# A two-block transformer kernel: bias tables of 384 keys issued from ScalarE's queue, and the activations at eight other distances from the weights

## The chip, the cores and the metric

The kernel runs on one core of a Trainium2 chip. The metric is the device time of one execution in microseconds (us); the kernel before was timed three times. On this core TensorE multiplies, VectorE (DVE), ScalarE (ACT) and GpSimd (POOL) do elementwise work, and DMAs that the queues of SyncE (SP) and ScalarE issue bring the weights from HBM.

## The reference

The activations are 256 tokens by 2048 features, all in float32. Two blocks follow each other.

```python
def first_block(x, c, ...):            # one layer
    mod = silu(c) @ w_ada + b_ada      # 6 vectors of 2048: shifts, scales, gates
    h = rmsnorm(x, g_mix) * (1 + sc1) + sh1
    x = x + gt1 * hybrid_mixer(h, w_in, ..., w_out)          # pooling, 8-head attention, LRU
    h = rmsnorm(x, g_ffn) * (1 + sc2) + sh2
    x = x + gt2 * conv_glu_ffn(h, w_gate, w_up, ..., w_down) # 2048 -> 5632 -> 2048
    return rmsnorm(x, final_g)

def second_block(x, ...):              # two layers
    for l in range(2):
        qa, ka, va, qb, kb, vb, qc, kc, vc = split(rmsnorm(x) @ w_in[l])
        oa = window_attention(qa, ka, va, a_sink[l], t5_table)   # bias depends on key - query
        ob = neighborhood_attention(qb, kb, vb, b_rpb[l])        # bias depends on grid offsets
        oc = axial_global_attention(qc, kc, vc, ...)
        x = x + concat(rmsnorm(oa), rmsnorm(ob), rmsnorm(oc)) @ w_o[l]
        u = relu(rmsnorm(x) @ w_up[l])                           # 2048 -> 8192
        x = x + (u * u) @ w_down[l]                              # 8192 -> 2048
    return rmsnorm(x, norm_final)
```

Nearly all the work is in the products with weights, which are read once each. In `window_attention` the bias of head h for query q and key k is one number per key − query; in `neighborhood_attention` the 256 tokens are 4 rows of 64 columns and the bias depends on the row offset and the column offset.

## The kernel before

**Weights.** A `Unit` is 1024 columns of weights on 128 partitions (two k-tiles of 512 columns, or four of 256). It is loaded to one of 7 `raw` buffers by a DMA that SP issues (line 130), and then split: ScalarE copies it to `whi` in fp32r (line 136), VectorE subtracts to get `wlo` (line 137). There are 3 buffers each of `whi` and `wlo` (`HB`). `Ada` items load the modulation weights through the same `raw` buffers (lines 158 and 162), and VectorE accumulates them (line 171).

**Products.** `mm_b` (lines 332 to 334) does three matmuls for each 128 x 128 block of weights: `whi` against the high part of the activations, `whi` against their low part, `wlo` against the high part. The weights are the stationary operand (loaded by LDWEIGHTS), 256 tokens of activations are the moving one. So a unit is 24 matmuls and 24 weight loads, and each matmul has a new weight load. The moving operands are `xh`/`xl` (the residual stream), `uh`/`ul` (the first block's hidden layer), `u` (two tiles `u0`, `u1`, in each layer of the second block), `mb` and the `xn` tiles (parts of the mixers). `mm_a` (lines 347 to 349) has the roles exchanged: 256 or 512 columns of weights move past 128 tokens of `xh`/`xl`.

**Addresses.** In the built program all `whi` and `wlo` buffers start at byte 192 modulo 512 of a partition, and the 128-column blocks that a weight load reads are 512 bytes long, so every weight load starts at 192 modulo 512. Moving slices are 1024 bytes and start at the tile's own residue. Below, *distance* is the start of the moving operand minus that of the weights, modulo 512 bytes. Before, it is 480 for `xh` and `xl`, 0 for `uh`, `ul`, `u0` and `u1`, 320 for `mb`, 288 for the `xn` tiles; in `mm_a`, moving minus stationary, it is 32.

**Order.** `drive` walks a list of items. It issues the DMA of an item up to 7 `raw` buffers ahead, splits up to 3 units ahead, and then emits the matmuls. After each unit, `step` resumes every active generator once; a `yield` in a generator is thus one unit of TensorE's work. `bias_tables` is such a generator; it is started when the first `down` of the first FFN begins. All instructions of an engine run in the order in which they were emitted, a queue's DMAs too.

**Bias tables.** `bias_tables` writes, in DRAM, `bias_a` (8 heads x 256 queries x 256 keys) from a row of 511 numbers per head, by four DMAs of two heads whose rows each start one number earlier; and `bias_b` for each layer (8 x 256 x 256) by 16 DMAs of 64 x 64 blocks for 8 heads. SP issues them, three units apart (lines 1385 and 1395). In each attention layer `heads2` reads a head's table back to a `bias` tile of 128 x 2 x 256 (line 1562), adds the mask `near` on GpSimd for the b heads (line 1568), and the softmax adds it to the scores (line 1049).

Of the kernel before, what the change touches and what calls it, by code (L numbers as in the profile page):

```python
# [9 lines left out]
F32 = mybir.dt.float32  # L10
F32R = mybir.dt.float32r
AF = mybir.ActivationFunctionType
ALU = mybir.AluOpType
# [4 lines left out]
P = 128  # L18
S = 256
D = 2048  # L20
KT = D // P
# [16 lines left out]
CUT2 = 0, 4, 8, 16  # L38
WORD = "p0 p1 a0 a1 b0 b1 l0 l1 p2 l2 a2 b2 p3 l3 a3 b3 p4 l4 a4 b4"
RRATE = 1  # L40
AHRATE = 1.4
HRATE = 1
WINDOWS = (2, 4, 8, 16)
# [139 lines left out]
def flat(a):  # L183
    return a.rearrange("p a b -> p (a b)")
# [15 lines left out]
class Builder:  # L200
# [100 lines left out]
    def dump(self, name, ap):  # L301
        if name in self.dbg:
            self.nc.gpsimd.dma_start(self.dbg[name], ap)

    def open_pool(self, name):
        cm = self.tc.tile_pool(name=name, bufs=1, reuse_waits="tile")
        self.ph = cm.__enter__()
        self.ph_cm = cm
# [168 lines left out]
    def run(self):  # L477
        tc, nc, io = self.tc, self.nc, self.io
        with ExitStack() as es:
            es.enter_context(tc.manual_schedule())  # L480
            cp = self.cp = es.enter_context(tc.tile_pool(name="cp", bufs=1))
            self.st = es.enter_context(tc.tile_pool(name="st", bufs=1))
            self.ps = es.enter_context(tc.tile_pool(name="ps", bufs=1, space=PSUM))
            self.dr = es.enter_context(tc.tile_pool(name="dr", bufs=1, space=DRAM))
            self.params = cp.tile([P, NPAR], F32, name="params")
            self.ident = cp.tile([P, P], F32, name="ident")
            self.ones = cp.tile([P, P], F32, name="ones")
            self.mhalf = cp.tile([P, 2], F32, name="mhalf")
            self.zero = cp.tile([P, 1], F32, name="zero")
            self.mod = cp.tile([P, 96], F32, name="mod")  # L490
            self.cact = cp.tile([P, 16], F32, name="cact")
            self.gsc = cp.tile([P, 16], F32, name="gsc")
            self.fgg = cp.tile([P, 16], F32, name="fgg")
            self.x = cp.tile([P, KT, S], F32, name="x")
            self.xh = cp.tile([P, KT, S], F32R, name="xh")
            self.xl = cp.tile([P, KT, S], F32R, name="xl")
            self.X = (self.xh, self.xl)
            self.rbc = cp.tile([P, S], F32, name="rbc")
            self.acc = cp.tile([P, 512], F32, name="acc")
            self.rtok = cp.tile([P, 2], F32, name="rtok")  # L500
            self.dg = cp.tile([P, S], F32, name="dg")
            nc.scalar.dma_start(self.params, io["params"])
            nc.scalar.dma_start(self.ident, io["ident"])
            nc.vector.memset(self.ones, 1.0)
            nc.vector.memset(self.mhalf, -0.5)
            nc.vector.memset(self.zero, 0.0)
            self.apc = tc.tile_pool(name="ap", bufs=1, reuse_waits="tile")
            self.ap_ = self.apc.__enter__()
            self.mixer()
            if self.upto >= 2:  # L510
                self.ffn()
            self.lead()
# [529 lines left out]
    def softmax(self, b, sc, pr, bias, sink, free=None):  # L1042

        nc = self.nc
        mx, nm, sm, r = self.small(), self.small(), self.small(), self.small()
        init = BIGNEG if sink is None else sink
        for i in range(2):
            other = self.zero.to_broadcast([P, S]) if bias is None else bias[:, i, :]
            nc.vector.tensor_tensor_reduce(
                pr[:, i, :], sc[:, i, :], other, 1.0, init, ALU.add, ALU.max, mx[:, i : i + 1]  # L1050
            )
        nc.vector.tensor_scalar(nm, mx, -1.0, None, ALU.mult)
        self.put("a", b)
        if free:
            self.put("bias", free)
        yield
        yield
        for i in range(2):
            nc.scalar.activation(pr[:, i, :], pr[:, i, :], AF.Exp, bias=nm[:, i : i + 1], accum_out=sm[:, i : i + 1])
        if sink is not None:  # L1060
# [16 lines left out]
    def fox(self, h):  # L1077

        nc = self.nc
        while "fq" not in self.flags:  # L1080
            yield
        pr = yield from self.take("pr", [P, 2, S])
        for i in range(2):
            nc.gpsimd.tensor_scalar(pr[1][:, i, :], self.causal[:, i, :], self.fq[:, i, h : h + 1], 1.0, ALU.add, ALU.mult)
        b = yield from self.bank()
        sc = b[1].rearrange("p (a k) -> p a k", a=2)
# [4 lines left out]
            )  # L1091
            nc.tensor.matmul(sc[:, i, :], sel, self.fs, start=False, stop=True)
        yield
        yield from self.softmax(b, sc, pr[1], pr[1], None)
        pt = yield from self.take("pt", [P, 2, S])
        b = yield from self.bank()
        self.transpose_p(b[1], pr[1])
# [7 lines left out]
        b = yield from self.bank()  # L1105
        o = b[1][:, :S]
# [4 lines left out]
        if "win" not in self.flags:  # L1111
# [5 lines left out]
            b = None  # L1117
# [11 lines left out]
    def ffn(self):  # L1129
        nc, io = self.nc, self.io  # L1130
        wg, wu, wd = io["w_ffn_gate"][0], io["w_ffn_up"][0], io["w_ffn_down"][0]
        F = {}

        def start():
            self.open_pool("ffnp")
            self.slots["sg"] = deque(range(2))
            ph = self.ph
            F["uh"] = ph.tile([P, KT, S], F32R, name="uh")
            F["ul"] = ph.tile([P, KT, S], F32R, name="ul")
            self.rms_now([self.acc, self.sq], self.rbc)  # L1140
# [178 lines left out]
        for q in range(4):  # L1319
            p = self.prep(q, src, "g_ffn", 48, 64, "fp", "ffn")  # L1320
# [27 lines left out]
    def bias_tables(self):  # L1348
# [3 lines left out]
        def rest(n):  # L1352
            for _ in range(n):
                yield
# [21 lines left out]
        rb = []  # L1376
        for l in range(2):
            rb.append(dr.tile([56, 127], F32, name=f"rb{l}"))
            nc.sync.dma_start(rb[l], rows[l])
        self.bias_a = dr.tile([8, S, S], F32, name="bias_a")  # L1380
        self.bias_b = [dr.tile([8, S, S], F32, name=f"bias_b{l}") for l in range(2)]
        yield from rest(12)
        base = rd[0:1, 255:256]
        for h in range(0, 8, 2):
            nc.sync.dma_start(
                self.bias_a[h : h + 2],
                bass.AP(tensor=base.tensor, offset=base.offset + 511 * h, ap=[[511, 2], [-1, S], [1, S]]),
            )
            yield from rest(3)
        for l in range(2):  # L1390
            for r in range(4):
                for r2 in range(4):
                    o = r2 - r + 3
                    base = rb[l][o : o + 1, 63:64]
                    nc.sync.dma_start(
                        self.bias_b[l][:, r * 64 : (r + 1) * 64, r2 * 64 : (r2 + 1) * 64],
                        bass.AP(tensor=base.tensor, offset=base.offset, ap=[[7 * 127, 8], [-1, 64], [1, 64]]),
                    )
                    yield from rest(3)

    def layer(self, l):
        nc, io = self.nc, self.io
# [149 lines left out]
        def heads2(t, kind, g, table, sink, near, need, values, last):  # L1552
# [5 lines left out]
            bias = [None, None]  # L1558
            if table is not None:
                for a in range(2):  # L1560
                    bias[a] = yield from self.take("bias", [P, 2, S])
                    nc.sync.dma_start(bias[a][1], table(a).rearrange("(b p) k -> p b k", p=P))
                yield
                yield
            if near:
                for a in range(2):
                    n = flat(bias[a][1]).rearrange("p (a c) -> p a c", c=64)
                    nc.gpsimd.tensor_tensor(n, n, L["near"].unsqueeze(1).to_broadcast([P, 8, 64]), ALU.add)
            pr = []
            for a in range(2):  # L1570
                pr.append((yield from self.take("pr", [P, 2, S])))
# [9 lines left out]
            yield  # L1581
            soft = [
                self.softmax(bs[a], sc[a], pr[a][1], bias[a][1] if bias[a] else None, sink(a) if sink else None, bias[a])
                for a in range(2)
            ]
            while soft:
# [200 lines left out]
        def mid():  # L1787
            self.close_pool()
            self.open_pool(f"mlp{l}")
            L["u"] = [self.ph.tile([P, KT, S], F32R, name=f"u{i}") for i in range(2)]  # L1790
            if l == 1:
                L["out"] = self.ph.tile([P, 2, D], F32, name="outt")

# [131 lines left out]
```

## Time and profile before

| | us |
|---|---|
| median of 3 runs | 3380.19 |
| lowest and highest | 3378.25 and 3380.22 |
| profiled execution, its own time | 3380.27 |
| its span (first to last instruction) | 3378.5 |

The three runs lie within 0.06% of each other. In the span TensorE's matmuls are busy 97%, its weight loads 95%, VectorE 62%, ScalarE 46%, GpSimd 9%. Matmuls are pipelined, so a busy TensorE is read by the distance in time from one matmul's start to the next, not by its busy share.

### The profile page before, as it was taken

How to read it: one execution, taken by the hardware profiler on the slowest of the kernel's cores; microseconds unless marked ns; L12 is line 12 of the kernel's file. 1: busy time of each engine (PE TensorE's matmuls, PEld its weight loads, DVE VectorE, ACT ScalarE, POOL GpSimd, SP SyncE). 2: the span in 40 equal slices, each digit the busy share in tenths (PEclk: the TensorE clock that was granted, in tenths of full speed). 3: DMA queues.
4: the chain of work that ended last, by engine and by line, in shares of the span. 5: the costliest groups of instructions: out<-in, count | busy, mean ns of one | idle time of the engine just before them, and what ended most of it. 6: DMA issues, size and time to landing. Idle time of an engine off the chain costs nothing.

```text
span 3378.5 us, 63581 instructions
## 1 busy us (share of the span) xinstructions
PE 3279.3 (97%) x26612; PEld 3196.3 (95%) x26612; DVE 2096.3 (62%) x2661; ACT 1569.5 (46%) x2094; POOL 297.6 (9%) x250
## 2 busy tenths in 40 slices
PE   7989899989999999999999999999999999999998
PEld 6988899989999998889999999999889999999998
DVE  7898887636745568666545454556776655545453
ACT  4436345434434466655434343444764533333334
POOL 0022100000000033111000000002110200000001
PEclk9999999989999999999999999999999999999999
DMA  9987887649866654556666666665455666666663
GB/s 362 338 285 231 303 300 242 187 157 298 290 196 187 188 171 133 168 157 183 185 185 184 184 185 185 184 185 162 144 174 163 182 185 184 186 182 187 183 186 125
DMA packets 390719, 683.93 MB, mean 202 GB/s; under 512 B 40823, under 2 KB 97952, under 8 KB 390176
## 3 DMA queue, kind: packets, MB, share of 16 engines
q1 hardware_dynamic: 390144, 679.56, 65.2%
q8 instruction: 208, 3.41, 0.4%
q14 instruction: 79, 0.65, 0.1%
q10 hardware_dynamic: 288, 0.31, 0.0%
HBM read 677.62 MB, written 8.46 MB: 203 GB/s over the span
## 4 chain that ended last, share of the span: by engine, by line
PE 80%; DVE 3%; DMA 3%; ACT 2%; issue 2%; SPq 0%; POOL 0%; ACTq 0%; DVEq 0%; POOLq 0%
PE pg L332 25%; PE pg L334 25%; PE pg L333 25%; DVE wlo L137 1%; DMA raw<-in_w_ffn_up 1%; PE pa L1578 1%; PE pa L1613 1%; PE pa L1073 1%; ACT whi L136 1%; DVE ada L171 1%; PE pg L347 1%; PE pg L348 1%; PE pg L349 1%; DMA raw<-in_w_ada 0%; DMA raw<-in_w_out 0%
## 5 line engine op out<-in xcount | busy, mean ns | idle before, releaser
L137 DVE TENSOR_TENSOR wlo<-raw,whi 128x1024 fp32r<-128x1024 f32 x1064 | 1318.0, 1240 | 1148.5 <-ACT whi L136 1134.9
L136 ACT ACTIVATE whi<-raw 128x1024 fp32r<-128x1024 f32 x1064 | 1123.3, 1058 | 1607.8 <-PE pg L333 1307.0
L332 PE MATMUL pg<-xh,whi 128*128 128x256 f32 x5184 | 1479.1, 285 | 24.7 <-ACT whi L136 20.3
L334 PE MATMUL pg<-xh,wlo 128*128 128x256 f32 x5184 | 1466.1, 283 | 9.4 <-DVE wlo L137 9.3
L333 PE MATMUL pg<-xl,whi 128*128 128x256 f32 x5184 | 1465.5, 283 | 1.8 <-DVE xl L565 1.1
L332 PEld LDWEIGHTS pg<-xh,whi 128*128 128x128 f32 x5184 | 985.5, 190 | 41.9 <-ACT whi L136 21.9
L334 PEld LDWEIGHTS pg<-xh,wlo 128*128 128x128 f32 x5184 | 985.5, 190 | 13.1 <-DVE wlo L137 12.7
L333 PEld LDWEIGHTS pg<-xl,whi 128*128 128x128 f32 x5184 | 985.6, 190 | 5.8 <-DVE xl L565 2.3
L332 PE MATMUL pg<-u,whi 128*128 128x256 f32 x2048 | 579.9, 283 | 0.0
L334 PE MATMUL pg<-u,wlo 128*128 128x256 f32 x2048 | 579.5, 283 | 0.0
L333 PE MATMUL pg<-u,whi 128*128 128x256 f32 x2048 | 579.5, 283 | 0.0
L333 PEld LDWEIGHTS pg<-u,whi 128*128 128x128 f32 x2048 | 393.1, 192 | 0.0
L334 PEld LDWEIGHTS pg<-u,wlo 128*128 128x128 f32 x2048 | 393.1, 192 | 0.0
L332 PEld LDWEIGHTS pg<-u,whi 128*128 128x128 f32 x2048 | 393.1, 192 | 0.0
L171 DVE SCALAR_TENSOR_TENSOR ada<-raw,cact,ada 128x1024 f32<-128x1024 f32 x180 | 233.7, 1298 | 18.9 <-DMA raw<-in_w_ada 17.9
L397 POOL TENSOR_TENSOR acc<-acc,t 128x512 f32<-128x512 f32 (+1 forms) x73 | 95.9, 1327 | 1360.3 <-ACT t L396 1359.2
L334 PE MATMUL pg<-uh,wlo 128*128 128x256 f32 x704 | 199.3, 283 | 0.0
L332 PE MATMUL pg<-uh,whi 128*128 128x256 f32 x704 | 199.3, 283 | 0.0
L333 PE MATMUL pg<-ul,whi 128*128 128x256 f32 x704 | 199.2, 283 | 0.0
L1809 POOL TENSOR_TENSOR y<-y 128x1024 f32<-128x1024 f32 x32 | 61.7, 1927 | 1200.0 <-ACT u L1808 1200.0
L332 PEld LDWEIGHTS pg<-uh,whi 128*128 128x128 f32 x704 | 135.1, 192 | 0.9 <-issue 0.9
L334 PEld LDWEIGHTS pg<-uh,wlo 128*128 128x128 f32 x704 | 135.1, 192 | 0.2 <-DVE wlo L137 0.2
(310 smaller groups left out, 2559.1 us busy)
## 6 DMA issues: line engine op xcount, KB each, us to landing
raw<-in_w_up SPq DMA_DIRECT2D x256, 512.0 KB
raw<-in_w_down SPq DMA_DIRECT2D x256, 512.0 KB
raw<-in_w_ada SPq DMA_DIRECT2D x192, 512.0 KB
raw<-in_w_in SPq DMA_DIRECT2D x192, 512.0 KB
raw<-in_w_ffn_gate SPq DMA_DIRECT2D x88, 512.0 KB
raw<-in_w_ffn_up SPq DMA_DIRECT2D x88, 512.0 KB
raw<-in_w_ffn_down SPq DMA_DIRECT2D x88, 512.0 KB
raw<-in_w_o SPq DMA_DIRECT2D x64, 512.0 KB
```

The costliest lines, as they stand in the source:

```text
L136: b.nc.scalar.activation(hi[:, :n], self.raw[:, :n], AF.Copy)
L137: b.nc.vector.tensor_tensor(lo[:, :n], self.raw[:, :n], hi[:, :n].bitcast(F32), ALU.subtract)
L171: b.nc.vector.scalar_tensor_tensor(g["acc"], self.raw, cs, g["acc"], ALU.mult, ALU.add)
L332: mm(o, wh, xh[:, k0 + j, :], start=st, stop=False, skip_group_check=True)
L333: mm(o, wh, xl[:, k0 + j, :], start=False, stop=False, skip_group_check=True)
L334: mm(o, wl, xh[:, k0 + j, :], start=False, stop=last and j == u.nk - 1, skip_group_check=True)
L347: mm(o, xh[:, k, tok], wh, start=st, stop=False, skip_group_check=True)
L348: mm(o, xh[:, k, tok], wl, start=False, stop=False, skip_group_check=True)
L349: mm(o, xl[:, k, tok], wh, start=False, stop=last and j == u.nk - 1, skip_group_check=True)
L397: nc.gpsimd.tensor_tensor(acc, acc, t, ALU.add)
L1073: self.nc.tensor.transpose(ps[:, k * S + i * P : k * S + (i + 1) * P], pr[:, i, k * P : (k + 1) * P], self.ident)
L1809: nc.gpsimd.tensor_tensor(flat(y), flat(y), flat(y), ALU.mult)
```

## The change

It has two parts that touch each other only through time.

*Bias tables.* `bias_a` and `bias_b` become 8 x 128 x 384: for each of 128 queries a row of 384 keys, of which the first 128 queries of the sequence read columns 128 to 383 and the last 128 read columns 0 to 255 (`by` in `heads2`). `bias_a` is still written by four DMAs, now of 256 rows of 384 numbers where it was 512 rows of 256; `bias_b` by 12 DMAs a layer where it was 16. ScalarE's queue issues them, four units apart where it was three. The `bias` tile is 128 x 384, read by one row a partition.

*Distances.* In `run`, small constant tiles are moved between the large ones; `uh`, `ul` and the `u` tiles come from `skewed`, which takes a tile that starts at a multiple of 512 bytes, with some unused bytes in front. The new distances, from the addresses of the built program:

| moving operand | before | after |
|---|---|---|
| `xh` | 480 | 64 |
| `xl` | 480 | 448 |
| `uh`, `ul` (first block) | 0, 0 | 384, 416 |
| `u0`, `u1` (second block, layer 0) | 0, 0 | 128, 192 |
| `u0`, `u1` (second block, layer 1) | 0, 0 | 256, 352 |

`mb` and `xn` stay at 320 and 288.

```diff
+WRES = 192
+    def skewed(self, name, skew):
+        n = (WRES + skew) % 512 // 4
+        t = self.ph.tile([P, n + KT * S], F32R, name=name, align_bytes=512)
+        return t[:, n:].rearrange("p (k s) -> p k s", k=KT)
 ...
-            F["uh"] = ph.tile([P, KT, S], F32R, name="uh")
-            F["ul"] = ph.tile([P, KT, S], F32R, name="ul")
+            F["uh"] = self.skewed("uh", 384)
+            F["ul"] = self.skewed("ul", 416)
 ...
-        self.bias_a = dr.tile([8, S, S], F32, name="bias_a")
+        self.bias_a = dr.tile([8, P, 384], F32, name="bias_a")
 ...
-            nc.sync.dma_start(
+            nc.scalar.dma_start(
                 self.bias_a[h : h + 2],
-                bass.AP(tensor=base.tensor, offset=base.offset + 511 * h, ap=[[511, 2], [-1, S], [1, S]]),
+                bass.AP(tensor=base.tensor, offset=base.offset + 511 * h, ap=[[511, 2], [-1, P], [1, 384]]),
             )
-            yield from rest(3)
+            yield from rest(4)
 ...
-            for r in range(4):
-                for r2 in range(4):
+            for r in range(2):
+                for m in range(6):
 ...
-                    bias[a] = yield from self.take("bias", [P, 2, S])
+                    bias[a] = yield from self.take("bias", [P, 384])
 ...
-            L["u"] = [self.ph.tile([P, KT, S], F32R, name=f"u{i}") for i in range(2)]
+            L["u"] = [self.skewed(f"u{i}", ((128, 192), (256, 352))[l][i]) for i in range(2)]
```

The distances change no instruction's place in its engine's order. The bias tables do. These rows are SP's queue of before, where the first block's FFN goes from its first `down` (`in_w_ffn_down`) to the next `gate`/`up` units; `raw` is a weight buffer, `rd` the rows of 511 numbers.

```order
L130 DMA raw<-in_w_ffn_down 128x2x512 x9
L130 DMA raw<-in_w_ffn_gate 128x2x512
L158 DMA raw<-in_w_ada 128x1024
L130 DMA raw<-in_w_ffn_gate 128x2x512
L1385 DMA bias_a<-rd 512x1x256
L130 DMA raw<-in_w_ffn_gate 128x2x512
L158 DMA raw<-in_w_ada 128x1024
L130 DMA raw<-in_w_ffn_gate 128x2x512
L1385 DMA bias_a<-rd 512x1x256
L130 DMA raw<-in_w_ffn_gate 128x2x512
L158 DMA raw<-in_w_ada 128x1024
```

And SP's queue of the change at the same place: only weights are left.

```order
L132 DMA raw<-in_w_ffn_down 128x2x512 x9
L132 DMA raw<-in_w_ffn_gate 128x2x512
L160 DMA raw<-in_w_ada 128x1024
L132 DMA raw<-in_w_ffn_gate 128x2x512 x2
L160 DMA raw<-in_w_ada 128x1024
L132 DMA raw<-in_w_ffn_gate 128x2x512 x2
L160 DMA raw<-in_w_ada 128x1024
```

The four `bias_a` DMAs have left the weights' queue. These rows are ScalarE's of the change, in the same stretch of the program: `whi<-raw` is the copy of a unit's weights, `y` a partial sum of `down`, `sg` the gate.

```order
L138 ACTIVATE whi<-raw 128x1024 x8
L1256 ACTIVATE y_7483<-pg 128x512 x2
L138 ACTIVATE whi<-raw 128x1024 x3
L1394 DMA bias_a<-rd 256x1x384
L138 ACTIVATE whi<-raw 128x1024 x4
L1394 DMA bias_a<-rd 256x1x384
L138 ACTIVATE whi<-raw 128x1024
L1256 ACTIVATE y_7734<-pg 128x512 x2
L138 ACTIVATE whi<-raw 128x1024 x3
L1394 DMA bias_a<-rd 256x1x384
L138 ACTIVATE whi<-raw 128x1024 x4
L1394 DMA bias_a<-rd 256x1x384
```

Each `bias_a` DMA now stands between two of ScalarE's weight copies, four of them apart, and the 24 DMAs of `bias_b` follow in the same way; before, ScalarE had only the copies here.

## Rows read from the trace of the kernel before

**Rows 1.** The page, part 1: busy time and share by engine.

```profile
PE 3279.3 (97%) x26612; PEld 3196.3 (95%) x26612; DVE 2096.3 (62%) x2661; ACT 1569.5 (46%) x2094; POOL 297.6 (9%) x250
```

**Rows 2.** The page, part 5: groups of matmuls: count, busy us, mean ns, idle before.

```profile
L332 PE MATMUL pg<-xh,whi 128*128 128x256 f32 x5184 | 1479.1, 285 | 24.7 <-ACT whi L136 20.3
L332 PE MATMUL pg<-u,whi 128*128 128x256 f32 x2048 | 579.9, 283 | 0.0
L332 PE MATMUL pg<-uh,whi 128*128 128x256 f32 x704 | 199.3, 283 | 0.0
```

**Rows 3.** Timeline, PE: first and last of 99 matmuls with `xh`/`xl`.

```profile
1939.61 0.28 PE L333 MATMUL pg<-xl,whi 128*128 128x256 f32 x1
...
1951.20 0.28 PE L332 MATMUL pg<-xh,whi 128*128 128x256 f32 x1
```

**Rows 4.** Timeline, PE: first and last of 99 matmuls with `u`.

```profile
1849.72 0.28 PE L333 MATMUL pg<-u,whi 128*128 128x256 f32 x1
...
1861.48 0.28 PE L332 MATMUL pg<-u,whi 128*128 128x256 f32 x1
```

**Rows 5.** Timeline, PE: first and last of 99 matmuls with `mb`.

```profile
1549.60 0.28 PE L333 MATMUL pg<-mb,whi 128*128 128x256 f32 x1
...
1561.14 0.28 PE L332 MATMUL pg<-mb,whi 128*128 128x256 f32 x1
```

**Rows 6.** Timeline, PE: first and last of 99 matmuls with `xn`.

```profile
349.83 0.28 PE L333 MATMUL pg<-xn,whi 128*128 128x256 f32 x1
...
361.26 0.28 PE L332 MATMUL pg<-xn,whi 128*128 128x256 f32 x1
```

**Rows 7.** Timeline, PE: first and last of 70 matmuls of `mm_a`, 256 columns.

```profile
2339.44 0.28 PE L349 MATMUL pg<-whi,xl 128*128 128x256 f32 x1
...
2347.49 0.27 PE L349 MATMUL pg<-whi,xl 128*128 128x256 f32 x1
```

**Rows 8.** Timeline, PE: first and last of 9 such matmuls of `mm_a`, earlier.

```profile
1275.54 0.42 PE L348 MATMUL pg<-wlo,xh 128*128 128x256 f32 x1
...
1277.25 0.41 PE L347 MATMUL pg<-whi,xh 128*128 128x256 f32 x1
```

**Rows 9.** Windows: busy us (count) by engine, granted clock, DMA share, GB/s.

```profile
690.00:720.00 30.00, 30.00 (x253) 30.00 (x252) 13.54 (x12) 13.46 (x15) 0.00 (x0) 1.00 0.48 147
720.00:780.00 60.00, 41.37 (x276) 39.96 (x275) 23.42 (x26) 15.04 (x17) 0.00 (x0) 0.80 0.57 189
780.00:820.00 40.00, 40.00 (x341) 40.00 (x340) 29.93 (x30) 17.74 (x19) 0.00 (x0) 1.00 0.96 316
...
1274.50:1277.50 3.00, 3.00 (x13) 2.48 (x12) 2.74 (x3) 2.03 (x5) 0.00 (x0) 0.50 0.08 12
```

**Rows 10.** Windows of line 332 alone: TensorE's busy us and count.

```profile
0.00:480.00 480.00, 244.11 (x848) 162.78 (x848) 0.96 0.88 304
```

**Rows 11.** Timeline, SP: DMA issues of the stretch with `bias_a`.

```profile
699.05 0.67 SPq L1385 DMA_DIRECT2D bias_a<-rd  x1
701.51 5.93 SPq L130 DMA_DIRECT2D raw<-in_w_ffn_gate  x1
...
710.15 13.62 SPq L130 DMA_DIRECT2D raw<-in_w_ffn_gate  x1
...
726.22 15.13 SPq L158 DMA_DIRECT2D raw<-in_w_ada  x1
...
744.45 15.84 SPq L130 DMA_DIRECT2D raw<-in_w_ffn_up  x1
```

**Rows 12.** Waits between 690 and 790 us: total, times, longest.

```profile
PE pg L332 <- ACT whi L136: 16.9, 3, 7.6
...
ACT whi L136 <- DMA raw<-in_w_ffn_gate: 13.5, 3, 11.7
```

**Rows 13.** Timeline, ScalarE and VectorE: the split of one unit.

```profile
1851.48 1.06 ACT L136 ACTIVATE whi<-raw 128x1024 fp32r<-128x1024 f32 x1 [1.82 <-PE pg L333]
1852.57 1.22 DVE L137 TENSOR_TENSOR wlo<-raw,whi 128x1024 fp32r<-128x1024 f32 x1 [1.66 <-ACT whi L136]
```

More of the change, by code (lines that the diff above doesn't have):

```diff
@@ L488, in run @@
             self.mhalf = cp.tile([P, 2], F32, name="mhalf")
-            self.zero = cp.tile([P, 1], F32, name="zero")
-            self.mod = cp.tile([P, 96], F32, name="mod")
             self.cact = cp.tile([P, 16], F32, name="cact")
@@ L495, in run @@
             self.xh = cp.tile([P, KT, S], F32R, name="xh")
+            self.mod = cp.tile([P, 96], F32, name="mod")
             self.xl = cp.tile([P, KT, S], F32R, name="xl")
+            self.zero = cp.tile([P, 1], F32, name="zero")
+            self.rtok = cp.tile([P, 2], F32, name="rtok")
             self.X = (self.xh, self.xl)
@@ L499, in run @@
             self.acc = cp.tile([P, 512], F32, name="acc")
-            self.rtok = cp.tile([P, 2], F32, name="rtok")
             self.dg = cp.tile([P, S], F32, name="dg")
@@ L1047, in softmax @@
         for i in range(2):
-            other = self.zero.to_broadcast([P, S]) if bias is None else bias[:, i, :]
+            other = self.zero.to_broadcast([P, S]) if bias is None else bias(i)
             nc.vector.tensor_tensor_reduce(
@@ L1093, in fox @@
         yield
-        yield from self.softmax(b, sc, pr[1], pr[1], None)
+        yield from self.softmax(b, sc, pr[1], lambda i: pr[1][:, i, :], None)
         pt = yield from self.take("pt", [P, 2, S])
@@ L1379, in bias_tables @@
             nc.sync.dma_start(rb[l], rows[l])
-        self.bias_a = dr.tile([8, S, S], F32, name="bias_a")
-        self.bias_b = [dr.tile([8, S, S], F32, name=f"bias_b{l}") for l in range(2)]
+        self.bias_a = dr.tile([8, P, 384], F32, name="bias_a")
+        self.bias_b = [dr.tile([8, P, 384], F32, name=f"bias_b{l}") for l in range(2)]
         yield from rest(12)
-        base = rd[0:1, 255:256]
+        base = rd[0:1, 127:128]
         for h in range(0, 8, 2):
-            nc.sync.dma_start(
+            nc.scalar.dma_start(
                 self.bias_a[h : h + 2],
-                bass.AP(tensor=base.tensor, offset=base.offset + 511 * h, ap=[[511, 2], [-1, S], [1, S]]),
+                bass.AP(tensor=base.tensor, offset=base.offset + 511 * h, ap=[[511, 2], [-1, P], [1, 384]]),
             )
-            yield from rest(3)
+            yield from rest(4)
         for l in range(2):
-            for r in range(4):
-                for r2 in range(4):
[L1393 to L1396, printed above, removed]
+            for r in range(2):
+                for m in range(6):
+                    base = rb[l][m + 1 - r : m + 2 - r, 63:64]
+                    nc.scalar.dma_start(
+                        self.bias_b[l][:, r * 64 : (r + 1) * 64, m * 64 : (m + 1) * 64],
                         bass.AP(tensor=base.tensor, offset=base.offset, ap=[[7 * 127, 8], [-1, 64], [1, 64]]),
                     )
-                    yield from rest(3)
+                    yield from rest(4)
     def layer(self, l):
@@ L1560, in heads2 @@
                 for a in range(2):
-                    bias[a] = yield from self.take("bias", [P, 2, S])
-                    nc.sync.dma_start(bias[a][1], table(a).rearrange("(b p) k -> p b k", p=P))
+                    bias[a] = yield from self.take("bias", [P, 384])
+                    nc.sync.dma_start(bias[a][1], table(a))
                 yield
@@ L1566, in heads2 @@
                 for a in range(2):
-                    n = flat(bias[a][1]).rearrange("p (a c) -> p a c", c=64)
-                    nc.gpsimd.tensor_tensor(n, n, L["near"].unsqueeze(1).to_broadcast([P, 8, 64]), ALU.add)
+                    n = bias[a][1].rearrange("p (a c) -> p a c", c=64)
+                    nc.gpsimd.tensor_tensor(n, n, L["near"].unsqueeze(1).to_broadcast([P, 6, 64]), ALU.add)
             pr = []
@@ L1581, in heads2 @@
             yield
+            by = lambda t: (lambda i: t[1][:, P - P * i : P - P * i + S]) if t else None
             soft = [
-                self.softmax(bs[a], sc[a], pr[a][1], bias[a][1] if bias[a] else None, sink(a) if sink else None, bias[a])
+                self.softmax(bs[a], sc[a], pr[a][1], by(bias[a]), sink(a) if sink else None, bias[a])
                 for a in range(2)
```

## The prediction

> **What bounds the kernel now.** I read the shares of busy time first: TensorE's matmuls and weight loads are busy 97% and 95%, VectorE 62%, ScalarE 46% [rows 1]. So the end is set by how fast one matmul follows another, and by the stretches where TensorE has nothing to do. Busy time per matmul (about 283 ns [rows 2]) does not tell the pace, since matmuls overlap; the timeline does, by the starts. I took stretches with one kind of moving operand, and divided the time from first to last start by the steps between.
>
> - `xh`/`xl`, distance 480: 11.59 us over 98 steps, 118.3 ns [rows 3].
> - `u`, distance 0: 11.76 us over 98 steps, 120.0 ns [rows 4].
> - `mb`, distance 320: 11.54 us over 98, 117.8 ns [rows 5].
> - `xn`, distance 288: 11.43 us over 98, 116.6 ns [rows 6].
> - `mm_a`, distance 32, roles exchanged: 8.05 us over 69, 116.7 ns [rows 7].
>
> The shape is the same in all five: 128 columns of weights, 256 moving columns. The pace differs by up to 3.4 ns, and all stand well above what the same `mm_a` matmuls show when the granted clock is half, the 1.2 GHz level: 1.71 us over 8 steps is 213.8 ns [rows 8, 9], half of which is 106.9 ns. If nothing else held them at 2.4 GHz, they would follow each other at that. So 10 to 13 ns of each matmul are lost to something that grows with the clock, and how much seems to go with the distance.
>
> The second thing is a stall. From 720 to 780 us TensorE starts 276 matmuls, at a granted clock of 0.80; the 30 us before have 253 [rows 9], one each 118.6 ns, at which 60 us would hold 506. The 230 that are missing are 27 us. The waits name the chain: TensorE for ScalarE's `whi`, ScalarE for a weight DMA, 11.7 us at the longest [rows 12]. SP's timeline says why that DMA is late: each of the four `bias_a` issues takes 0.6 to 0.7 us, but the weight issue behind it holds SP for 5.9, 13.6, 15.1 and 15.8 us [rows 11], 50.5 us in all. DMA engines are only 57% busy there [rows 9]: it is a queue that stands, not bandwidth that is used up.
>
> **The change, part by part.** *Distances of x.* 15,552 matmuls (3 x 5184 [rows 2]; lines 333 and 334 have the counts of 332) go from 480 to 64 and 448. No row shows either distance. The nearest rows are 32 (116.7) and 480 (118.3). Since the four distances other than 0 lie between 116.6 and 118.3, with no order in them that I can extend, I take their mean, 117.4, for all eight new ones. Before 480 us the loads set the pace (DMA share 0.88 [rows 10]), so I count only what follows: 3 x (5184 − 848) = 13,008. Times 0.9 ns: 12 us saved. *Distances of u.* 3 x 2048 + 3 x 704 = 8256 matmuls [rows 2] leave 0, the slowest. TensorE is not idle before any of those of line 332 [rows 2], so nothing hides the gain. Times 2.6 ns: 21 us saved. The bounds of both: 106.9 ns on one side (x −148 us, u −108 us). On the other, no better than distance 0: x at 120.0 costs 22 us, u saves nothing.
>
> Here the Trainium skill speaks against the change. "TensorE: Matmul & The Clock Gate", step 1 of its Step-by-step section, gives TensorE two independent SBUF read ports, one for the moving operand and one for LDWEIGHTS, and says that loading the next weights does not take read bandwidth from the running matmul. By that the distance could do nothing and both terms would be 0. The rows [rows 3 to 7] disagree so far: one shape, five paces.
>
> *Bias tables off SP's queue.* Now no weight stands behind a `bias_a` on SP's queue, so the 50.5 us of held issues lose their cause. The same DMA engines still carry it, in 256 rows of 384 numbers for 512 of 256: three quarters of the bytes, half the pieces. Weights and tables will share the engines, and the next stretch runs them at 0.96 [rows 9] while it fills the buffers again, so I return 20 of the 27 us. Bound above: 27. Bound below: a loss. If the queue stands for ScalarE as it did for SP, ScalarE is held instead, and behind it are the weight copies that TensorE needs. How much can it bear? A copy begins at 1851.48, when TensorE frees the buffer, and `wlo` is there at 1853.79 [rows 13], 2.3 us on; two more units of 24 x 0.120 = 2.9 us are ready, so 3.4 us are spare. Holds of 5.9, 13.6, 15.1 and 15.8 us less 3.4 each are 37 us, 10 more than now.
>
> *ScalarE's 28 issues.* At 0.67 us each, as `bias_a`'s on SP [rows 11], 19 us, one in four units, each inside the 3.4 us spare. 0; if that cover were gone, 19 us. *Smaller tables.* Each read has three quarters of the bytes, GpSimd adds the mask on 384 columns instead of 512. Nothing on TensorE waits for it: 0. *`mm_a`* has other distances too (64 and −64 mod 512 for 32), but only 384 matmuls: at 3 ns 1 us, 0.
>
> The sum, against the profiled execution's own 3380.3 (span 3378.5 and 1.8 around it; the median of the runs is 0.1 lower): 3380.3 − 12 − 21 − 20 = **3327 us**.
>
> **The rivals.** *A. The distance is not the cause.* The five paces belong to five places in the program, and each keeps its own. For it: in this trace tile and distance never change apart. Against: `u`, `mb`, `xn` and `xh`/`xl` use the same three lines, weight buffers and shape. Only the tables change the time: 3380 − 20 = 3360. The page on TensorE named above gives this result.
>
> *B. Some distances are far better.* 116.6 is the best of four drawn without aim; the floor of 106.9 is 10 ns below. If the new ones on average lie as far below 116.6 as that lies below 120.0, at 113.2, x saves 66 us and u 56: 3380 − 122 − 20 = 3238. For it: eight new draws. Against: the spread of four was only 1.7 ns.
>
> *C. ScalarE is held.* Four issues 11.4 us apart (four units) against the 13 to 16 us that SP was held: the third or fourth finds the queue full. Cost as above, +10 for −20: 3380 − 33 + 10 = 3357. For it: the four holds. Against: half as many pieces. "DMA: Bandwidth & Descriptors" of the Trainium skill, section "Issuing engines are not separate DMA queues", leans this way: DMAs of all issuing engines run on the same 16 DMA engines, and another issuer saves only the sequencer's time. No run here yet shows a large DMA on ScalarE's queue.
>
> *D. x gets a bad distance, and the kernel is slower.* `u` shows a distance at which the pace is the worst of all. x has the most matmuls and the shortest way to fall. At 120.9 (as far above 118.3 as the mean of the good ones lies below 120.0) with u unchanged at 120.0, x costs 2.6 x 13,008 = 34 us: 3380 + 34 − 20 = 3394. It decides from 119.8 on, where 1.5 ns x 13,008 eats the 20 us of the tables. For it: nothing shows 64 or 448. Against: all four measured distances other than 0 are below 118.4.
>
> **How the numbers follow.** My forecast 0.58, A 0.08, B 0.10, C 0.14, D 0.10. The forecast's own range is 3300 to 3354: 1.25 ns of pace on the 21,264 matmuls counted is 27 us, and the 10 to 27 us that the tables may return lie within that. To hold 8 in 10 it has to take in A and most of C above, and below the part of B in which the mean is near 115.5 ns: 3285 to 3365 us. A difference below 0.2% (7 us) is about what a measurement of this kernel cannot tell from none. Faster: the forecast, A, B and most of C, 0.88. Same: what is left of C and the middle of D, 0.06. Slower: the rest of D, 0.06.
>
> **What the changed profile would show.** The paces: in the second block the `up` units (x) and the `down` units (u, two distances a layer) can be read apart by the starts in the timeline; right if x is near 117.4 and each `down` is below 120.0, wrong if they stay at 118.3 and 120.0 (A), or if x is above 119.8 (D). The stall: TensorE should start about 500 matmuls in the 60 us after the first `bias_a` DMA, at a granted clock near 1.0, and no weight issue of SP should last over 6 us there; if ScalarE's DMA issues last several us and TensorE waits for `whi`, C is right. What would make the number wrong above all is the pace at 64, since two thirds of x's matmuls have it: 1 ns there is 9 us.

## The result and the profile after

The changed kernel takes 3342.95 us (median of 4 runs, 3340.76 to 3344.11), the kernel before 3380.2 beside it (one of its four runs there, slow at 3548.8 us, is left out of the ratio). The ratio is 0.9891, 95% interval [0.9872, 0.991]: 37 us less, where 53 were forecast. The profiled execution takes 3343.74 us, its span is 3341.9.

The first row is the page's part 1 of the changed kernel, which answers to [rows 1]: the shares hardly move, as they must on a kernel whose TensorE stays the bound.

```profile
PE 3256.0 (97%) x26612; PEld 3172.6 (95%) x26612; DVE 2092.3 (63%) x2661; ACT 1568.9 (47%) x2094; POOL 294.2 (9%) x250
```

The windows of the changed kernel, with the columns of [rows 9], for the 60 us from the first `bias_a` DMA on, and for the 60 us that stand where 720 to 780 us stood:

```profile
697.40:757.40 60.00, 56.31 (x467) 55.13 (x466) 33.37 (x34) 23.88 (x26) 0.00 (x0) 1.00 0.66 221
718.30:778.30 60.00, 55.89 (x462) 54.51 (x461) 40.12 (x42) 23.63 (x25) 0.00 (x0) 1.00 0.73 263
```

That is 462 matmuls where [rows 9] have 276, at a granted clock of 1.00 where it was 0.80; in the 60 us from its own first `bias_a` DMA on, the kernel before has 343. The stall is mostly gone, not wholly: at 117.6 ns each 60 us would hold 510.

ScalarE's timeline of the changed kernel has the four issues that took the place of SP's in [rows 11], and behind them SP's, between 731 and 744 us:

```profile
697.41 1.20 ACTq L1394 DMA_DIRECT2D bias_a<-rd  x1
708.72 0.60 ACTq L1394 DMA_DIRECT2D bias_a<-rd  x1
720.03 0.58 ACTq L1394 DMA_DIRECT2D bias_a<-rd  x1
731.34 0.58 ACTq L1394 DMA_DIRECT2D bias_a<-rd  x1
```

```profile
731.32 0.62 SPq L132 DMA_DIRECT2D raw<-in_w_ffn_up  x1
743.35 0.37 SPq L132 DMA_DIRECT2D raw<-in_w_ffn_up  x1
```

No issue of either queue is held: ScalarE's longest is 1.2 us, and none of SP's from 690 to 790 us reaches 2 us, where [rows 11] have 5.9 to 15.8. But the weights still wait for the tables. Between the two SP rows SP issues nothing for 11.4 us, and SP's own waits from 690 to 790 us (total, times, longest) say for what; the kernel before has no wait of this kind there:

```profile
SPq L132 <- DMA bias_a<-rd: 23.2, 2, 11.8
...
SPq L160 <- DMA bias_a<-rd: 9.3, 1, 9.3
```

In this program the DMAs of both queues take turns on eight semaphores, and a weight DMA is issued only when the earlier DMA on its semaphore has landed. By the trace's semaphore records the weight DMA of 743.35 shares its semaphore with the table DMA that ScalarE issued at 720.03, and that one landed at 743.28, 23 us after its issue. So the tables have left the weights' queue, but weights are held by the landing of the tables.

What is left of the stall stands in the waits of the changed kernel from 690 to 790 us. ScalarE waits 13.9 us for `gate` and `up` weights; before it was 13.5 for `gate` alone, with a longest of 11.7 [rows 12], and 12.0 for `up`. TensorE waits 2.7 us for `wlo`, and 1.4 for `whi`, where it was 16.9 [rows 12]:

```profile
ACT whi L138 <- DMA raw<-in_w_ffn_up: 10.7, 4, 5.0
ACT whi L138 <- DMA raw<-in_w_ffn_gate: 3.2, 2, 2.9
...
PE pg L342 <- DVE wlo L139: 2.7, 4, 0.8
...
PE pg L340 <- ACT whi L138: 1.4, 2, 1.2
```

The paces are read as in [rows 3] and [rows 4], first and last of 99 matmuls. TensorE's timeline of the changed kernel: `xh`/`xl` at two places, then `uh`/`ul`, `u` of layer 0, and `u` of layer 1.

```profile
540.65 0.28 PE L340 MATMUL pg<-xh,whi 128*128 128x256 f32 x1
...
552.18 0.28 PE L342 MATMUL pg<-xh,wlo 128*128 128x256 f32 x1
...
1941.64 0.28 PE L340 MATMUL pg<-xh,whi 128*128 128x256 f32 x1
...
1953.11 0.28 PE L342 MATMUL pg<-xh,wlo 128*128 128x256 f32 x1
...
904.69 0.28 PE L340 MATMUL pg<-uh,whi 128*128 128x256 f32 x1
...
916.23 0.28 PE L342 MATMUL pg<-uh,wlo 128*128 128x256 f32 x1
...
1812.82 0.28 PE L340 MATMUL pg<-u,whi 128*128 128x256 f32 x1
...
1824.68 0.28 PE L342 MATMUL pg<-u,wlo 128*128 128x256 f32 x1
...
2700.00 0.28 PE L342 MATMUL pg<-u,wlo 128*128 128x256 f32 x1
...
2711.55 0.28 PE L341 MATMUL pg<-u,whi 128*128 128x256 f32 x1
```

Divided by 98: x 117.7 and 117.0 ns, `uh`/`ul` 117.8, layer 0 **121.0**, layer 1 117.9. Layer 0's two new distances are worse than the 120.0 of [rows 4]. Over all steps of these lines shorter than 145 ns in the trace (x from 480 us on):

| moving operand | steps | before, ns | after, ns | us |
|---|---|---|---|---|
| `xh`, `xl` | 13,117 | 118.33 | 117.55 | −10.2 |
| `uh`, `ul` | 2108 | 119.98 | 117.78 | −4.6 |
| `u`, layer 0 | 3072 | 119.98 | 121.09 | +3.4 |
| `u`, layer 1 | 3068 | 119.96 | 117.78 | −6.7 |
| `mb`, `xn` (distances unchanged) | 757 | 117.8, 116.7 | 117.8, 116.7 | 0 |

In the stretch of the tables, 690 to 840 us, the time that the other starts there take above 118 ns each falls from 27.6 to 5.8 us, −21.8. All else in the span is 3.1 us longer in the same count. Most of it lies between the 9000th and the 11,000th matmul, from 1208 to 1480 us in the kernel before, where the second block begins; what makes it was not followed further. The sum, −36.8, stands against −36.6 between the spans.

### The profile page after: what moved, and what is told of

Same layout as the page of the kernel before. It is cut to its first block, busy times and chain, and to the rows that moved or that the text cites. A ratio compares the mean times of both kernels' runs of the same rounds, so it can differ in the third digit from the quotient of the medians.

```text
span 3341.9 us, 63573 instructions
## 1 busy us (share of the span) xinstructions
PE 3256.0 (97%) x26612; PEld 3172.6 (95%) x26612; DVE 2092.3 (63%) x2661; ACT 1568.9 (47%) x2094; POOL 294.2 (9%) x250
## 4 chain that ended last, share of the span: by engine, by line
PE 78%; DVE 4%; DMA 3%; ACT 2%; issue 2%; POOL 0%; ACTq 0%; SPq 0%; DVEq 0%; POOLq 0%
PE pg L342 25%; PE pg L340 24%; PE pg L341 24%; DVE wlo L139 2%; ACT whi L138 1%; PE pa L1081 1%; DMA bias_a<-rd 1%; PE pa L1622 1%; DMA raw<-in_w_ada 1%; PE pa L1586 1%; DMA raw<-in_w_ffn_up 1%; DVE ada L173 1%; PE pg L355 0%; PE pg L357 0%; PE pg L356 0%
## 5 line engine op out<-in xcount | busy, mean ns | idle before, releaser
L342 PE MATMUL pg<-xh,wlo 128*128 128x256 f32 x5184 | 1466.4, 283 | 11.7 <-DVE wlo L139 11.5
L342 PEld LDWEIGHTS pg<-xh,wlo 128*128 128x128 f32 x5184 | 979.8, 189 | 16.2 <-DVE wlo L139 15.8
L340 PEld LDWEIGHTS pg<-u,whi 128*128 128x128 f32 x2048 | 386.4, 189 | 0.0
L341 PEld LDWEIGHTS pg<-u,whi 128*128 128x128 f32 x2048 | 385.4, 188 | 0.0
```

What stands on the lines that cost most here:

```text
L340: mm(o, wh, xh[:, k0 + j, :], start=st, stop=False, skip_group_check=True)
L341: mm(o, wh, xl[:, k0 + j, :], start=False, stop=False, skip_group_check=True)
L342: mm(o, wl, xh[:, k0 + j, :], start=False, stop=last and j == u.nk - 1, skip_group_check=True)
```

## The experiments

### Either part alone

The distances alone: the kernel before with the hunks on distances (`skewed` and its calls, the constant tiles in `run`). The tables alone: the kernel before with the hunks on tables.

> The eight distances of the changed kernel with the bias tables of the kernel before (256 x 256, issued by SP, three units apart). Theory (the pace goes with the distance): the paces of the changed kernel come back, x 117.55 ns, uh/ul 117.8, u of layer 0 121.1, u of layer 1 117.8; 13,008 x 0.8 + 2112 x 2.2 - 3072 x 1.1 + 3072 x 2.2 = 18 us less than before, 3362 us. TensorE starts under 300 matmuls in the 60 us from the first bias_a DMA on, as before. Rival (the paces moved because the tables' DMAs left SP's queue or because of something else in time): the paces of before, 118.3 and 120.0, and 3380 us.

> The tables of 384 keys issued by ScalarE, with the distances of before (480 for x, 0 for uh, ul and u). Theory: the paces are those of before, 118.3 and 120.0, and the stretch of the bias tables runs as in the changed kernel, over 450 matmuls in the 60 us from the first bias_a DMA on. What the two parts do adds up, so 3343 + 18 = 3361 us, with 17 to 20 us less than before. Rival (the two parts are worth something only together, or the tables give back next to nothing): 3375 us or more.

Distances alone: 3362.87 us (ratio 0.9951, [0.9934, 0.9967]), 17 us less than before. x 117.54 ns, `uh`/`ul` 117.78, layer 0 121.09, layer 1 117.78, as in the changed kernel within 0.02 ns, with the tables where they were. Tables alone: 3360.52 us (0.9941, [0.9926, 0.9956]), 19 us less; the paces are those of before (118.3 and 120.0), and TensorE starts 457 matmuls in the 60 us from the first `bias_a` DMA, where the distances alone have 354 and the kernel before 343. (The expected "under 300" for the distances alone fits the window of [rows 9], not this one.) 17 + 19 are 36 of the 37: the parts hardly touch. The distance moves the pace, and the tables' DMAs do not. Rival A is out.

### The queue or the tables' size

The changed kernel with its tables on SP's queue, and the changed kernel with the large tables of before on ScalarE's:

```diff
-            nc.scalar.dma_start(            # small tables, both issues
+            nc.sync.dma_start(
 ...
-        self.bias_a = dr.tile([8, P, 384], F32, name="bias_a")       # large tables
+        self.bias_a = dr.tile([8, S, S], F32, name="bias_a")
             nc.scalar.dma_start(
 ...
             yield from rest(4)
```

> The changed kernel with one word changed at each of the two issues: SP issues the tables of 384 keys, four units apart, and ScalarE issues none. Theory 1 (it is the queue: whatever weight stands behind a table on the same queue waits for it): weight issues of SP behind a bias_a last 5 to 15 us again, TensorE starts 280 to 380 matmuls in the 60 us, and 15 to 20 us of the gain are gone: 3358 to 3363 us. Theory 2 (it is the tables' size: three quarters of the bytes in half the pieces): no weight issue lasts over 6 us because of it, and the time stays within 4 us of the changed kernel's 3343.

> The changed kernel with the tables of before, 256 x 256 in 4 + 32 DMAs, issued by ScalarE four units apart. Theory 1 (the queue): about the changed kernel's 3343 us, at most 8 us more for the larger traffic, no weight issue of SP held over 6 us by a bias_a; if ScalarE is held by its own issues, its DMA issues last several us and TensorE waits for whi. Theory 2 (the size): the stall of before is back, under 350 matmuls in 60 us, and 3358 us or more.

Small tables on SP: 3348.97 us (0.9907, [0.9892, 0.9922]), 6 us above the changed kernel, though the weight issues behind a `bias_a` are held again, 2.8, 8.0 and 9.2 us. Large tables on ScalarE: 3356.93 us (0.9932, [0.9917, 0.9947]), 14 us above. So of the 20 us that lie between large tables on SP (3363, the distances alone) and the changed kernel, the smaller tables on SP's queue give 14, and the other queue with large tables gives 6. Both theories fall in their pure form, and the size is worth more than the queue. (With the size goes the spacing, four units for three. No run parts these two, but the run of the next section keeps three units and has no stall.)

The second run shows rival C at work. ScalarE's timeline of the kernel with large tables on its queue:

```profile
698.42 1.19 ACTq L1393 DMA_DIRECT2D bias_a<-rd  x1
709.73 2.08 ACTq L1393 DMA_DIRECT2D bias_a<-rd  x1
721.04 9.66 ACTq L1393 DMA_DIRECT2D bias_a<-rd  x1
735.97 12.04 ACTq L1393 DMA_DIRECT2D bias_a<-rd  x1
```

And its waits from 690 to 790 us:

```profile
ACT whi L138 <- issue: 19.8, 2, 11.1
PEld pg L340 <- ACT whi L138: 12.1, 4, 5.0
PE pg L340 <- ACT whi L138: 11.3, 4, 4.8
```

The third and fourth issue hold ScalarE for 9.7 and 12.0 us, the copies to `whi` behind them are late, and TensorE waits. SP, which no issue holds for as much as 1 us there, waits 51.8 us for `bias_a` DMAs to land. ScalarE's hold is the mechanism, and it begins at the issue, that rival C named; the smaller tables kept it away (1.2 us at most).

### What the size stands for: two DMA engines

The packet records of the trace say why. In the kernel before, the 512 rows of one `bias_a` DMA take 46 to 51 ns each on average, some 25 us together, and run in 12.4 to 14.6 us: about two at a time, which is the outer dimension, two heads. The changed kernel's 256 rows take 66 ns each; on SP's queue one DMA runs in 8.1 to 11.1 us, again about two at a time, and on ScalarE's, beside the weights, in 12 to 16 us.

The semaphore records agree. In the kernel before, the last weight DMA ahead of the tables, issued at 698.63 us, raises its semaphore in 16 steps that all come within 0.3 us. Of the 16 steps of the weight DMA that was issued at 701.51, behind the first table, 14 come within 0.8 us, by 711.6, and the last two at 715.2 and 715.7. Each table DMA ends with two such steps. So one part in eight of a weight load stands behind the table's rows, and the load is done only with that part.

So the same large tables, on the same queue, were cut along queries instead of heads:

```diff
-        for h in range(0, 8, 2):
+        for q in range(0, S, 64):
             nc.sync.dma_start(
-                self.bias_a[h : h + 2],
-                bass.AP(tensor=base.tensor, offset=base.offset + 511 * h, ap=[[511, 2], [-1, S], [1, S]]),
+                self.bias_a[:, q : q + 64, :],
+                bass.AP(tensor=base.tensor, offset=base.offset - q, ap=[[511, 8], [-1, 64], [1, S]]),
```

> The distances of the changed kernel and the large tables of before on SP's queue, three units apart, but each of the four bias_a DMAs writes 64 queries of all 8 heads instead of 256 queries of 2 heads: as many rows of 256 numbers, as many bytes, the same queue. Theory 1 (what holds the weights is that the 512 rows of one DMA go through two of the 16 DMA engines one after another, 12 to 14 us, and a weight DMA is done only when its share on these two is): with 8 engines the rows take about 512 x 0.046 / 8 = 3 us, no weight issue lasts over 6 us, and most of the 28 us stall is gone, 3337 to 3348 us. Theory 2 (it is the bytes, the count of rows or SP's queue itself): as with the large tables on SP's queue, 3363 us.

3337.39 us (0.9874, [0.986, 0.9889]), as its first theory had it: 26 us under the same kernel with two heads a DMA, and 6 under the changed kernel. The 512 rows now run in 3.0 to 5.2 us, five to eight at a time; a table DMA ends with eight steps of its semaphore, and the 16 of the weight DMA behind the first table come within 0.7 us. Windows of this kernel, 60 us from the first `bias_a` DMA on:

```profile
698.30:758.30 60.00, 60.00 (x512) 60.00 (x511) 38.99 (x38) 26.74 (x29) 0.00 (x0) 1.00 0.88 286
```

512 starts, the full number, and no issue over 2 us on SP, which carries all the tables. The Trainium skill has this rule: "DMA: Bandwidth & Descriptors", section "Rules for kernel authors", says that a DMA whose outermost dimension is smaller than 16 is confined to at most that many of the engines. The trace agrees: about 2 rows at a time with 2 outside, 5 to 8 with 8.

### Equal pairs of distances

Here both parts of an operand stand at one distance, so that a pace can be given to it (the changed kernel otherwise):

```diff
-            F["uh"] = self.skewed("uh", 384)    # a: 384, 384   b: 416, 416   c: 32, 32
-            F["ul"] = self.skewed("ul", 416)
-  ((128, 192), (256, 352))[l][i]                # a: (128, 128), (256, 256)
-                                                # b: (192, 192), (352, 352)   c: (64, 64), (192, 192)
-  xh, mod, xl                                   # a: xh, xl, mod (64, 64)   b: mod, xh, xl (448, 448)
```

> The changed kernel with both parts of each pair at one distance: xh, xl 64; uh, ul 384; u of layer 0 128, 128; u of layer 1 256, 256. Theory 1 (a step's length depends on the distance of the operand that moves in it, and the two neighbours only shift it a little): the paces are the means of the steps of the changed kernel in which that distance moved, x 118.1, uh/ul 117.4, layer 0 119.8, layer 1 117.9 ns; 13,008 x 0.55 - 2112 x 0.4 - 3072 x 1.3 = +2 us on the changed kernel's 3343, 3345 us. Theory 2 (it is the difference between the two parts that counts, so a pair with equal parts paces like the equal pairs of before): 116.6 to 118.3 in all four places, layer 0 too; 3330 to 3343 us.

> The same with the other distance of each pair: xh, xl 448; uh, ul 416; u of layer 0 192, 192; u of layer 1 352, 352. Theory 1: x 116.5, uh/ul 118.5, layer 0 123.7, layer 1 117.6 ns; 3343 - 13,008 x 1.05 + 2112 x 0.7 + 3072 x 2.6 - 3072 x 0.2 = 3338 us. Theory 2: 116.6 to 118.3 in all four places, layer 0 too, and 3325 to 3335 us.

> The changed kernel with uh, ul at 32, 32, u of layer 0 at 64, 64 and u of layer 1 at 192, 192; x stays at 64 and 448. It puts a distance in another place: 64 (so far x's) in layer 0, 192 (so far layer 0's) in layer 1, 32 (so far mm_a's) in the first block. Theory 1 (the distance sets the pace, wherever it stands): layer 0 is at the 118.1 of x's steps at 64, layer 1 at the 123.7 of layer 0's steps at 192, uh/ul at mm_a's 116.7; 3343 - 2112 x 1.1 - 3072 x 3.0 + 3072 x 5.9 = 3350 us. Rival (layer 0 is slow for another reason than its distances): layer 0 stays at 120 or more, layer 1 at 118.

| kernel | us | ratio | x | `uh`/`ul` | layer 0 | layer 1 |
|---|---|---|---|---|---|---|
| a | 3346.4 | 0.990 [0.9886, 0.9915] | 64: 117.64 | 384: 118.66 | 128: 118.66 | 256: 119.99 |
| b | 3294.78 | 0.9747 [0.9733, 0.9762] | 448: 114.69 | 416: 118.36 | 192: 113.33 | 352: 119.97 |
| c | 3315.98 | 0.981 [0.9793, 0.9826] | 64 and 448: 117.48 | 32: 116.68 | 64: 117.78 | 192: 113.35 |

Run a ended at its expected 3345 by accident: layer 1 was about 2 ns and `uh`/`ul` 1.3 ns worse than the first theory had them, layer 0 1.1 and x half a nanosecond better. Runs b and c ended 43 and 34 us under the first theory. Both theories fall, and so does run c's rival: layer 0 is not slow by its place. 192, which moved in the slowest steps of the changed kernel (the matmuls of `whi` with the second part of layer 0's `u`, 123.7 ns), is at 113.3 when both parts have it; 256 and 352, at 120.0 each alone, make 117.78 together. A distance has no pace by itself: the two parts of the pair, which move in turn, set it together. The 114.69 of 448 is no pace either but a mean of two: of x's runs of 24 steps in run b from 480 us on, 320 are at 113.3 to 114.5 and 118 at 117.5 to 118.0. (64 twice, in run a, has 113.3 in 3 of 441.) In `u` it is the pair and not the place: 192 twice is 113.3 in layer 0 and in layer 1, as TensorE's timeline shows, first of run b in layer 0:

```profile
1796.44 0.28 PE L340 MATMUL pg<-u,whi 128*128 128x256 f32 x1
...
1807.54 0.28 PE L342 MATMUL pg<-u,wlo 128*128 128x256 f32 x1
```

and of run c in layer 1:

```profile
2700.07 0.28 PE L340 MATMUL pg<-u,whi 128*128 128x256 f32 x1
...
2711.17 0.28 PE L342 MATMUL pg<-u,wlo 128*128 128x256 f32 x1
```

### All at 192, and the map

Three kernels with x at 192, 192 and the tables of 384 keys on SP's queue, 32 queries of all 8 heads a DMA; in the first all other `u` parts are at 192 as well.

```diff
+            cp.tile([P, 32], F32, name="pad")
             self.xh = cp.tile([P, KT, S], F32R, name="xh")
-            self.mod = cp.tile([P, 96], F32, name="mod")
             self.xl = cp.tile([P, KT, S], F32R, name="xl")
+            self.mod = cp.tile([P, 96], F32, name="mod")
+            cp.tile([P, 96], F32, name="pad2")
 ...
+                self.bias_a[:, q : q + 32, :],
+                bass.AP(tensor=base.tensor, offset=base.offset - q, ap=[[511, 8], [-1, 32], [1, 384]]),
```

> All of xh, xl, uh, ul and u at distance 192 (x by 512 unused bytes around it, which leaves the weights at 192 modulo 512), and the tables of 384 keys on SP's queue, each bias_a DMA with 32 queries of all 8 heads. Theory 1 (an equal pair at 192 paces at 113.35 ns in every place, as in layer 0 and in layer 1 so far, and a table DMA that is cut over 8 engines holds no weight): against the changed kernel x saves 13,008 x 4.2 = 55 us, uh/ul 2112 x 4.4 = 9, layer 0 3072 x 7.7 = 24, layer 1 3072 x 4.4 = 14, the tables 7; 3343 - 109 = 3234 us, up to 15 us more if, at the faster pace, the splits and the loads end later than TensorE needs them: 3234 to 3249. Theory 2 (x is held by something else too, since its equal pair at 448 is at 114.7 and not at 113.35): x at 114.7, 3252 to 3267 us.

> The kernel with all at 192, but uh, ul at 96, 96, u of layer 0 at 160, 160 and u of layer 1 at 224, 224. Theory 1 (for an equal pair the pace repeats every 256 bytes of distance, as 0 and 256 at 120.0, 32 and 288 at 116.7, 64 and 320 at 117.7, 128 and 384 at 118.7 suggest): 96 as 352, 120.0; 160 as 416, 118.4; 224 as 480, 118.3 ns. Theory 2 (no such period; 192 and 448 differ by 1.3 ns already): at least one of the three is over 1 ns away from these. By theory 1 the time is that of the kernel with all at 192 plus 2112 x 6.6 + 3072 x 5.0 + 3072 x 5.0 = 45 us.

> The kernel with all at 192, but uh, ul at 192 and 448, u of layer 0 at 192 and 128 (the changed kernel's two in the other order), u of layer 1 at 192 and 0. Theory 1 (what counts is each part modulo 256 and the difference of the two parts): 192 and 448 pace as an equal pair, 113.4 to 114.7 ns; 192 and 128 are as slow as 128 and 192, near 121; 192 and 0 lie above 117. Theory 2 (each step by the distance that moves in it, of equal pairs): uh/ul 113.8, layer 0 (2 x 113.35 + 118.7) / 3 = 115.1, layer 1 (2 x 113.35 + 120.0) / 3 = 115.6 ns.

All at 192: **3264.23 us** (0.966, [0.9644, 0.9676]), 79 us under the changed kernel, the best of this study, with no stall at the tables. The second theory's number came: both layers' `u` at 113.3, but x at 114.70 and `uh`/`ul` at 115.93 on average. Its reason, something else that holds x, did not: x too runs at 113.3 for long. In runs of 24 steps x has a mean of 113.3 to 114.5 (359 runs) or of 117.5 to 118.0 (142), and none between. TensorE's timeline: first and last of 99 matmuls at 800 us, a break at 1545, and first and last of 99 at 1560:

```profile
800.07 0.28 PE L340 MATMUL pg<-xh,whi 128*128 128x256 f32 x1
...
811.61 0.28 PE L342 MATMUL pg<-xh,wlo 128*128 128x256 f32 x1
...
1544.95 0.60 PE L455 MATMUL pa<-dg,ones 128*128 128x256 f32 x2
1545.19 0.47 PE L340 MATMUL pg<-xh,whi 128*128 128x256 f32 x1
...
1556.73 0.28 PE L341 MATMUL pg<-xl,whi 128*128 128x256 f32 x1
...
1567.84 0.28 PE L340 MATMUL pg<-xh,whi 128*128 128x256 f32 x1
```

The same operands at the same distance take 117.8 ns a step at the one place and 113.4 at the other. Within a row of matmuls on one operand that is not broken, no change of pace was found in this trace; it comes where the row is broken, by other matmuls as at 1544.95 or by a wait, or where another operand follows. From 1545 to 2233 us 6071 matmuls follow each other at 113.3 ns without a change. So a pair allows several rhythms, and it seems that the way in which TensorE comes out of a break chooses one. x and `uh`/`ul` in the first block come out into the slower one more often: 162 of 291 runs of 24, against 29 of 292 for x in the second block. The x of the changed kernel, at 117.7 and 117.0 above, has two rhythms as well.

The map kernel takes 3296.33 us (0.9757, [0.9737, 0.9776]), 32 above all at 192 where 45 were expected; pairs at 96, 160 and 224 pace at 119.98, 117.33 and 118.32. 96 is as 352 and 224 as 480, but 160 is 1.0 ns from 416's mean, enough for the second theory by its own terms. Its ground is gone, though, since 448's 114.7 is 113.3 and 117.8 mixed, as with 192. The period of 256 holds by and large, and what it leaves may be rhythms: 416's runs of 24 lie from 117.0 to 119.0, and 160's at 117.0 to 117.5. The kernel of pairs takes 3297.51 us (0.976, [0.9741, 0.978]): 192 with 448 at 115.94, as 192 twice in that place (115.93), which speaks for the period as well; 192 with 128 at 118.88, not the 121.09 of 128 with 192, so it counts which part has which distance (the first moves in two of three steps); 192 with 0 at 119.03. Of the first theory the first pair came as the equal pair there, though above the 113.4 to 114.7 that it named, the second missed by 2 ns, and the third came. The second theory was off by 2 to 4 ns on all three.

## Why the prediction was right, and where not

The time fell within the range, 16 us above the forecast. The distances were worth 18 us where 33 were forecast, the tables 19 to 22 where 20 were; for the tables the cause was half wrong, and the size came out partly by luck.

*x, −12 us.* Right: −10 us. A mean of 117.4 was assumed for the pair, 117.55 was found. The reason given for it, that 64 and 448 pace like any other, was not a good one, and here luck helped: 448 twice spends most of its steps at 113.3, and together with 64 that is lost. The number was expected to hang on the pace at 64; it hung on layer 0's `u`.

*u, −21 us.* This is the mis-sized term: −8 us. "I take their mean, 117.4, for all eight new ones" was 0.4 off for `uh`/`ul` and layer 1, but 3.7 for layer 0, at 121.09, where the sign asked for was a pace below 120.0. "On the other, no better than distance 0" was no bound: a pair exists that is worse than distance 0 and than either of its parts twice. 13 of the 16 us between forecast and result are this term, 2 are x.

*Bias tables, −20 us.* The size was right: −19 alone, and 467 matmuls start in the 60 us where about 500 were asked for. But it was right by luck in part. The step that failed is the cause that the prediction gave: "it is a queue that stands", so that leaving SP's queue was the cure. The queue is where the wait is seen. The cause was a DMA with two heads outside, whose rows run two at a time. Another queue with the large tables gave 6 us; the smaller tables, which had no price of their own, gave 14 of the 20 even on SP's queue, and tables cut along queries on SP's queue left no stall. In the changed kernel itself the held issues are gone, as predicted, but SP waits 32.5 us for `bias_a` DMAs to land (23.2 and 9.3 above). "Three quarters of the bytes, half the pieces" stood in the prediction as a remark; it was most of the term.

*ScalarE's issues, the table reads, `mm_a`: 0.* Not shown one by one. The 3.1 us that the rest of the span lost are the most that the balance has for them; no issue of ScalarE lasts over 1.2 us.

*The rivals.* A (place, not distance) is refuted by the run of the distances alone: operands at other addresses, and nothing else, made 17 us. By the rule of the Trainium skill that was weighed there, "TensorE: Matmul & The Clock Gate", step 1 of its Step-by-step, a weight load takes no read bandwidth from the running matmul. The prediction drew from it that the addresses could do nothing; the measured 17 us decide against that. Whether it is the weight load's reads that cost the time is not shown, since every matmul here has one. B (distances far better, 113.2) was not what happened, but such a pair exists: 192 twice, at 113.33 ns; in the changed kernel 192 is paired with 128, where it is of no use. C was kept away by the smaller tables, and appeared with the large ones. D happened in layer 0 instead of x, where it costs 3 us.

*What stays open.* Why the two parts of a pair act on each other, and what chooses a rhythm at a break, is not known: only the start addresses were varied here, with the weights at 192 throughout, so that a distance from the weights cannot be told from the operand's own address modulo 512. That the second block's long stretches hold one rhythm, and the first block's mix two, is an observation.

## What to carry to other kernels

When matmuls follow each other with a new weight load each, measure the steps start to start, and try the start addresses of the moving operands, both parts together: here all operands at one good distance were worth some 90 us (an estimate: 3264 against 3337 + 17, which the distances of before would make with tables cut along queries), and one pair mixed from the best distance and another was the worst of all. Look at single stretches too: a mean can hide two rhythms. A DMA with an outer dimension of two ran about two rows at a time here; the large one held what stood behind it on its queue, SP's or ScalarE's, and the weights waited for the landing of either from the other queue. Cut it so that the outer dimension is large before moving it to another queue.

## What the runs showed that was not expected

At the 2.4 GHz level the paces that come back most are 113.3, 117.8 and 120.0 ns for 256 columns, that is 272, 283 and 288 cycles; at the half clock the same shape takes 213.8 ns [rows 8], 257 cycles of 1.2 GHz. By that the best pair still loses some 15 cycles a matmul.

The rhythm can also change in a place that nobody touched. `xn` stands at distance 288 in every kernel, and its steps take 116.7 to 116.8 ns in all but one; in run a of the equal pairs seven of its eight runs of 24 take 120.0, and its mean is 118.26.
